# A hybrid encoder layer: V stored once in token order, stores of attention results moved to another queue, the first norm placed elsewhere

## The chip, the core and the metric

The kernel runs on one core of a Trainium2 chip. A core has five engines that run their own instruction streams side by side and wait for each other by semaphores: TensorE (PE: matrix products and transposes, with its weight load shown as PEld), VectorE (DVE), ScalarE (ACT), GpSimd (POOL) and SyncE (SP). Data moves between DRAM and the on-chip memory by DMA; in this kernel DMAs are issued by SP and, for some stores, by ACT. Each engine takes its instructions in order, and a DMA issue that has to wait holds up what stands behind it on the engine that issues it. PE writes to eight banks of a small accumulation memory (PSUM), from which DVE and ACT fetch the results.

The metric is the device time of one launch in microseconds (us).

## The reference

One encoder layer with one batch of 2048 tokens and 1024 features, in float32:

```python
y = rmsnorm(h, norm_mix_g) @ w_in                      # q, k, v: 8 heads of 64; a, g: 512 each
att = dilated_sliding_attention(rot(q), rot(k), v)     # three patterns, mixed by their denominators
conv = silu(layernorm(depthwise_conv31(a * sigmoid(g))))
h = h + concat([att, conv]) @ w_out
h = h + cross_attention(rmsnorm(h), rmsnorm(mem))      # 4 heads of 256, 256 memory rows
h = h + square(relu(rmsnorm(h) @ w_up)) @ w_down       # 4096 wide
out = rmsnorm(h, norm_final_g)
```

The three patterns are `(128, 1), (512, 4), (2048, 16)`: in each, a token attends to those up to 64 steps away on both sides, where a step is 1, 4 or 16 tokens. The results of the three patterns are added with weights that come from a softmax over their log-denominators.

## The kernel before

Every matrix product is made of three: each operand is split into a high part that PE takes exactly and a low remainder, and `mm3` (L204) adds high x high, high x low and low x high. The splitting is the work of ACT (`ACT.copy`) and DVE or POOL (the subtraction). With a free size of 512 such a product is 24 matmuls for 1024 rows of weights.

The program goes through these stages:

- Up to about 230 us: the products of the memory rows with the cross attention's weights, and the normalised transposed x, kept as high and low parts for four quarters of 512 tokens.
- Up to about 405 us: the projections of q and k (`lin_qk`) and the gated input of the convolution (`glu`, for the first two quarters of the tokens). Beside them `vscale` (L517) computes a scale for every 128 features of V: it sums squares of the weights on POOL (L526, L527), and in the next step PE adds them up over partitions (L533). Each `yield` is a place where `weave` may give another generator its turn; `vscale` has two for each of its four rounds, and a rate of 0.3 rounds per step of the main line.
- 405 to 557 us: `lin_v` (L543), V for two groups of four heads in 16 tiles of 128 tokens each, with `glu` between and after. A tile is 24 matmuls, an ACT cast to half precision (L571), a DVE subtraction (L572) and stores. A row of V (`VR`, 1040 half-precision numbers) has for each head 64 high parts, two ones and 64 low parts. The tile `vst` (8 buffers) goes to DRAM three times, once for each pattern in the order in which the pattern reads it: `vscr3` by one DMA from SP, `vscr2` by four from ACT, `vscr1` by two from SP, so seven DMAs for each tile.
- About 557 to 905 us: attention of quarter 0 (`att(0, p2_)`, L1029). Pattern 3 (step 16) is done here for the whole sequence (`att_far`), patterns 1 and 2 for the first quarter. Into this stage are woven the first layer norm of the convolution (`conv_ln(0)`, L1030: one of its steps after each of the first nine steps of attention) and then the rest of `glu` for the last two quarters (`rest`, 0.8 steps per step of attention).
- After that, for each of the four quarters, `post(p)`: output projection, cross attention, MLP and final norm, with the attention of the next quarter and its convolution woven in.

Attention works in units. A far unit (`att_far.unit`, L820) takes four of the 16 residues of one head: PE writes scores to two banks (L829, L830), DVE adds the mask and takes the minimum into column 65 of the result tile (`att_probs`, L762), ACT exponentiates (L763); a step later PE transposes (L769), ACT and DVE split into high and low (L772, L773); a step later PE multiplies with V (L777 to L779), DVE or ACT copies the result (L841, L839) and SP stores it to `oscr` (L842). `att` (L989) keeps three units in flight and takes two steps of the woven generators for each. The result tile of a far unit is `o3` with three buffers, so a unit can't begin to write its minimum before the store of the third unit before it has landed. A near unit does the same with pattern 2 (`pat` 1) and pattern 1 (`pat` 0); the result of pattern 2 for a pair of heads (`o1`, one buffer) is stored by SP (L962), that of pattern 1 stays on the chip.

When a pair of heads is through, `combine` (L851) loads the stored results of patterns 2 and 3 back (`ld`, by two DMAs from SP), waits two steps and then mixes them on DVE, POOL and ACT. At the same time `load_v` (L916) fetches V for the next pair of heads: one DMA for pattern 3 (in quarter 0 only), two for pattern 2, one for pattern 1; each of these tiles has one buffer. `far_keys` (L802) loads the keys of a head for pattern 3 as a whole, 16 x 160 with edges; `far_q` (L807) loads the high and the low part of q, and POOL copies the high part to the other 64 partitions.

The order of the instructions on each engine is not simply that of the program text: a planner in the framework simulates the program and puts each engine's instructions in an order by its own estimates of when they are ready. `pinned` and `after` (L78, L83) tell it to issue a step's work not before a named earlier instruction.

`conv_ln` (L225) takes the tiles that its caller gives it through `alloc`; for the first norm these are the eight buffers `t2`, which `glu` uses too.

Of the kernel before, what the change touches and what calls it, by code (L numbers as in the profile page):

```python
# [47 lines left out]
def hybrid_layer(ctx, tc, A, out):  # L48
# [61 lines left out]
    vscr1 = dr.tile([17, 16, 8, VR], F16, name="vscr1")  # L110
    vscr2 = dr.tile([4, 5, 4, 32, VR], F16, name="vscr2")
    vscr3 = dr.tile([16, P, VR], F16, name="vscr3")
# [404 lines left out]
    def vscale():  # L517

        for pr in range(4):
            sq = [t2(f"vsq{pr}{q}", F32, (P, 4, P)) for q in range(2)]  # L520
            for q in range(2):
                dma(sq[q], wcols(w_in, 2 * DATT + P * pr, rows=(4 * q, 4 * q + 4)))
            for k in range(KC):
                w = sq[k // 4][:, k % 4]
                ACT.activation(w, w, AF.Square, scale=gain("mix", k))
            POOL.tensor_tensor(sq[0], sq[0], sq[1], op=ALU.add)  # L526
            POOL.tensor_tensor(sq[0][:, 0:2], sq[0][:, 0:2], sq[0][:, 2:4], op=ALU.add)  # L527
            yield
            with ExitStack() as st:
                after(st, "pe", "dve")  # L530
                pc = ps("c", f"vss{pr}")
                for q in range(2):
                    PE.matmul(pc[:, 0:1], sq[0][:, q], ones[:, 0:1], start=q == 0, stop=q == 1)  # L533
                v = top.tile([P, 4], F32, tag="vs", name=f"vs{pr}", bufs=2)
                DVE.tensor_scalar(v[:, 0:1], pc[:, 0:1], 1e-30, None, op0=ALU.max)
                POOL.tensor_tensor(v[:, 1:2], v[:, 0:1], mhalf, op=ALU.pow)
                DVE.tensor_scalar(v[:, 2:3], v[:, 1:2], 512.0, None, op0=ALU.mult)
                DVE.tensor_scalar(vmul[:, pr:pr + 1].bitcast(I32), v[:, 2:3].bitcast(I32), 0x7F800000, None,
                                  op0=ALU.bitwise_and)
                DVE.reciprocal(vinv[:, pr:pr + 1], vmul[:, pr:pr + 1])  # L540
            yield

    def lin_v(g, ns):  # L543
# [18 lines left out]
        for t in range(4 * ns[0], 4 * ns[-1] + 4):  # L562
# [5 lines left out]
            st = lbv.tile([P, 4, VW], F16, tag="vst", name=f"vst{g}_{t}", bufs=8)  # L568
# [6 lines left out]
            dma(vscr3[:, 8 * t:8 * t + 8, gs].rearrange("r i e -> i r e"), s2)  # L575
            c2, i2 = divmod(PADI + 8 * t, 32)
            for b in range(4):
                dma(vscr2[b, c2, :, i2:i2 + 8, gs].rearrange("a i e -> i a e"), s2[b:P:4], nc.scalar)
            for e in range(2):
                dma(vscr1[t + e, :, 4 - 4 * e:8 - 4 * e, gs].rearrange("r i e -> i r e"), s2[64 * e:64 * e + 64])  # L580
# [116 lines left out]
    def edges():  # L697
        zrow = wp.tile([16, 1, VR], F16, tag="raw", name="zrow", bufs=2)
        DVE.memset(zrow, 0.0)
        zb = zrow.to_broadcast([16, 4, VR])  # L700
        for b in range(4):
            dma(vscr2[b, 0, :, 0:PADI, :].rearrange("a i e -> i a e"), zb)
            dma(vscr2[b, 4, :, PADI:, :].rearrange("a i e -> i a e"), zb)
        dma(vscr1[0, :, 0:4, :], zb)
        dma(vscr1[16, :, 4:8, :], zb)
# [24 lines left out]
    with ExitStack() as st:  # L730
        lbk = pool("lin_k", stack=st)
        cu = pool("conv0", stack=st)
        conv0 = pinned(conv_units(cu, 0, (0, 1)), "dve")
        weave(islice(steps, 31), (vsc, 0.3), (conv0, 0.5))
        drain(vsc, conv0)
        next(steps)
# [65 lines left out]
    def far_keys(p2_, h):  # L802
        k = p2_.tile([P, 16, 160], F32R, tag="k3", name=f"k3_{h}", bufs=2)
        dma(f(k.rearrange("p r i -> p (r i)")), f(kscr[:, :, h].rearrange("x d r i -> (x d) (r i)")))
        return k

    def far_q(h, e):  # L807
# [3 lines left out]
        for x, d in ((0, t), (1, ql)):  # L811
            dma(f(d[0:64]), f(qfar[x, :, h, 8 * e:8 * e + 8, :].rearrange("d r i -> d (r i)")))
        POOL.tensor_copy(t[64:P], f(t[0:64]))
        return t, ql

    def att_far(p2_, h, k, vt, q):

        pr, hh = divmod(h, 2)

        def unit(rq, qh, ql):  # L820
            os_ = p2_.tile([P, 4, ROW], F32, tag="o3", name=f"o3_{h}{rq}", bufs=3)
# [20 lines left out]
            dma(oscr[pr][1].rearrange("(p r) (h e) -> p r h e", r=16, h=2)[:, 4 * rq:4 * rq + 4, hh], os_)  # L842
# [8 lines left out]
    def combine(p, pr, o0):  # L851
# [6 lines left out]
        yield  # L858
        sm_ = top.tile([P, 5, 8], F32, tag="csm", name=f"csm{p}{pr}")
# [49 lines left out]
    def att_units(p, far, then):  # L909
# [6 lines left out]
        def load_v(pr):  # L916
            es = slice(pr * 2 * VW, (pr + 1) * 2 * VW)
            if far:
                vt[2] = far.tile([P, 16, 2 * VW], F16, tag="v3", name=f"v3_{pr}")
                dma(vt[2], vscr3[:, :, es].rearrange("r i e -> i r e"))  # L920
            vt[1] = aq.tile([P, 4, 2, 2 * VW], F16, tag="v2", name=f"v2_{p}{pr}")
            for c in range(2):
                dma(vt[1][:, :, c], vscr2[:, p + c, :, :, es].rearrange("b a i e -> (a i) b e"))
            vt[0] = aq.tile([P, 5, 2 * VW], F16, tag="v1", name=f"v1_{p}{pr}")
            dma(vt[0], vscr1[4 * p:4 * p + 5, :, :, es].rearrange("c r i e -> (r i) c e"))

        def unit(pr, hh, pat, g, k, q_, os_, opt):
# [33 lines left out]
            if g and hh and pat:  # L961
                dma(oscr[pr][0][512 * p:512 * (p + 1)].rearrange("(p b) e -> p b e", b=4),  # L962
                    os_.rearrange("p b h e -> p b (h e)"))
# [53 lines left out]
    with ExitStack() as st:  # L1017
        p2_ = pool("att_far", stack=st, side="right")
        p2_.tile([P, 16, 160], F32R, tag="k3", name="k3", bufs=2)
        qlow3 = low_parts(p2_, 1024, 2, "ql3")  # L1020
        p2_.tile([P, 200], F32, name="farpad")
# [3 lines left out]

        def ln_alloc(role, dtype, name, shape=(P, 512)):
            return top.tile(list(shape), F32, tag="cl_" + role, name=name) if role[:3] == "col" else t2(name, dtype)

        first = pinned(att(0, p2_), "pe")  # L1029
        weave(islice(first, 9), (pinned(conv_ln(0, ln_alloc), "pe"), 1))  # L1030
        weave(first, (rest, 0.8))
# [291 lines left out]
```

## Time and profile before

| what | value |
|---|---|
| median of three runs | 3071.7 us (3071.03 to 3072.67) |
| the profiled execution's own time | 3069.8 us |
| its span, from the first to the last instruction | 3068.0 us |
| PE busy | 2908.4 us (95% of the span) |
| DVE, ACT, POOL busy | 1853.8, 1198.6, 416.9 us |
| mean granted clock of PE | 0.973 |
| DMA packets and data | 612871, 440.54 MB |

The profile is one execution of the program, recorded by the hardware. A line of the page names the engine, the line of the kernel (L205 is line 205), the tile that is written and those that are read; a wait names the instruction or the DMA that ended it. SPq and ACTq are the issues of DMAs by these engines, with the time that an issue took on the engine. Matmuls are pipelined and overlap, so the distance between starts tells more than the length of one. The page cuts the span into 40 slices of 76.7 us and gives the busy share of each in tenths; PEclk is the share of its full clock that PE was granted.

### The profile page before, as it was taken

The numbers are of one execution on the slowest core, as the hardware profiler recorded it, in microseconds if no ns is written. First come the engines' busy times: TensorE is split into PE (matmuls) and PEld (weight loads), VectorE is DVE, ScalarE is ACT, GpSimd is POOL, SyncE is SP. The second block draws the span as 40 slices with busy tenths as digits, with TensorE's granted clock in tenths as the row PEclk, the third lists the DMA queues.
The fourth block names the chain that finished last, engine by engine and source line by source line (L and its number), as shares of the span: only waits on it lengthen the run. The fifth ranks groups of instructions, "written<-read, shape, count | busy, mean of one in ns | idle before, by whom it ended". The sixth has DMA issues, their size and how long they took to land.

```text
span 3068.0 us, 43093 instructions
## 1 busy us (share of the span) xinstructions
PE 2908.4 (95%) x16396; PEld 2479.3 (81%) x16396; DVE 1853.8 (60%) x3295; ACT 1198.6 (39%) x2002; POOL 416.9 (14%) x486
## 2 busy tenths in 40 slices
PE   8989998677779999999999999999999999999999
PEld 8878798566668888888888888888888888988888
DVE  6545534344466777666768776666967656554445
ACT  5633211355533533343443344344433444432332
POOL 2336411212110011120001101100100120000000
PEclk9999999699889999999999999999999999999999
DMA  8878855556472444455434445453534355233332
GB/s 270 281 166 202 198 142 152 173 142 164 124 215 90 132 124 136 126 157 163 139 114 131 120 138 150 140 177 109 139 109 134 111 156 174 83 96 97 96 97 76
DMA packets 612871, 440.54 MB, mean 144 GB/s; under 512 B 191461, under 2 KB 541721, under 8 KB 611640
## 3 DMA queue, kind: packets, MB, share of 16 engines
q1 hardware_dynamic: 588056, 424.08, 48.5%
q10 hardware_dynamic: 24608, 13.71, 1.7%
q8 instruction: 129, 2.11, 0.3%
q14 instruction: 78, 0.64, 0.1%
HBM read 337.27 MB, written 100.42 MB: 143 GB/s over the span
## 4 chain that ended last, share of the span: by engine, by line
PE 72%; DMA 6%; DVE 5%; ACT 2%; issue 1%; ACTq 0%; SPq 0%; POOL 0%; POOLq 0%; DVEq 0%
PE dn L205 7%; PE up L205 7%; PE up L207 7%; PE up L206 7%; PE dn L207 7%; PE dn L206 7%; DMA vscr<-vst 3%; PE s L942 2%; PE pt L769 2%; PE xs L205 2%; PE xs L207 2%; PE xs L206 2%; PE x L205 2%; PE x L207 2%; PE x L206 2%; PE o L206 2%
## 5 line engine op out<-in xcount | busy, mean ns | idle before, releaser
L206 PE MATMUL dn<-hhl,whi_d 128*128 128x512 f32 (+1 forms) x1056 | 403.2, 384 | 2.8 <-DVE hhl L1201 2.8
L205 PE MATMUL up<-mh,whi_u 128*128 128x512 f32 x1024 | 402.3, 393 | 0.5 <-DVE rl L1198 0.5
L207 PE MATMUL dn<-hhh,wlo_d 128*128 128x512 f32 (+1 forms) x1056 | 402.7, 384 | 0.0
L205 PE MATMUL dn<-hhh,whi_d 128*128 128x512 f32 (+1 forms) x1056 | 400.4, 392 | 0.0
L207 PE MATMUL up<-mh,wlo_u 128*128 128x512 f32 x1024 | 399.3, 390 | 0.0
L206 PE MATMUL up<-ml,whi_u 128*128 128x512 f32 x1024 | 398.8, 389 | 0.0
L219 DVE SCALAR_TENSOR_TENSOR cacc<-cu,cw,cacc 128x512 f32<-128x512 f32 x480 | 384.1, 802 | 6.2
L196 ACT CAST whi_d<-raw_d 128x1024 fp32r<-128x1024 f32 x128 | 134.6, 1052 | 392.0 <-PE up L206 383.7
L1216 DVE TENSOR_TENSOR h<-h,dn 128x512 f32<-128x512 f32 (+1 forms) x264 | 172.2, 667 | 190.9 <-PE dn L207 190.3
L196 ACT CAST whi_u<-raw_u 128x1024 fp32r<-128x1024 f32 x128 | 134.6, 1052 | 371.3 <-PE dn L206 332.4
L763 ACT ACTIVATE sm<-sm,o 128x256 f32<-128x256 f32 (+1 forms) x384 | 172.7, 469 | 216.9 <-DVE o L762 213.6
L1198 DVE SCALAR_TENSOR_TENSOR rl<-up,ssumx 128x512 f32<-128x512 f32 x128 | 87.9, 690 | 238.6 <-PE up L207 235.2
L207 PEld LDWEIGHTS dn<-hhh,wlo_d 128*128 128x128 f32 x1056 | 198.5, 188 | 39.5
L206 PEld LDWEIGHTS dn<-hhl,whi_d 128*128 128x128 f32 x1056 | 198.8, 188 | 38.6 <-DVE hhl L1201 3.4
L205 PEld LDWEIGHTS dn<-hhh,whi_d 128*128 128x128 f32 x1056 | 198.0, 188 | 38.8 <-DVE h L1216 3.2
L207 PEld LDWEIGHTS up<-mh,wlo_u 128*128 128x128 f32 x1024 | 192.3, 188 | 39.9
L205 PEld LDWEIGHTS up<-mh,whi_u 128*128 128x128 f32 x1024 | 192.2, 188 | 38.6 <-DVE rl L1198 0.9
L206 PEld LDWEIGHTS up<-ml,whi_u 128*128 128x128 f32 x1024 | 192.5, 188 | 38.0
L762 DVE CUSTOM_DVE_ANT_0 sm<-s,mask 128x256 f32<-128x256 f32 (+1 forms) x384 | 139.9, 376 | 123.0 <-PE s L942 83.2
L197 DVE TENSOR_TENSOR wlo_d<-raw_d,whi_d 128x1024 fp32r<-128x1024 f32 x128 | 161.2, 1259 | 19.5 <-ACT whi_d L196 19.3
L197 DVE TENSOR_TENSOR wlo_u<-raw_u,whi_u 128x1024 fp32r<-128x1024 f32 x128 | 161.2, 1259 | 8.9 <-ACT whi_u L196 8.9
L205 PE MATMUL xs<-whi_a,yh 128*128 128x256 f32 x512 | 149.6, 293 | 8.8 <-ACT xp L1159 6.0
(386 smaller groups left out, 6575.3 us busy)
## 6 DMA issues: line engine op xcount, KB each, us to landing
raw_u<-in_w_up_dram SPq DMA_DIRECT2D x128, 512.0 KB
raw_d<-in_w_down_dram SPq DMA_DIRECT2D x128, 512.0 KB
raw_o<-in_w_out_dram SPq DMA_DIRECT2D x32, 512.0 KB
raw_a<-ascr SPq DMA_DIRECT2D x32, 512.0 KB
raw_b<-bscr SPq DMA_DIRECT2D x32, 512.0 KB
k<-kscr SPq DMA_DIRECT2D x24, 512.0 KB
k<-kscr SPq DMA_DIRECT2D x8, 1280.0 KB
ld<-oscr SPq DMA_DIRECT2D x32, 264.0 KB
```

The lines of the kernel that those rows point to most:

```text
L196: ACT.copy(hi, raw)
L197: (lo_eng or DVE).tensor_tensor(lo, raw, f(hi), op=ALU.subtract)
L205: PE.matmul(o, lh, rh, start=first, stop=False)
L206: PE.matmul(o, lh, rl, start=False, stop=False)
L207: last["pe"] = PE.matmul(o, ll, rh, start=False, stop=end)
L219: DVE.scalar_tensor_tensor(acc, u[:, t:t + 512], cw[:, c, t:t + 1], acc, op0=ALU.mult, op1=ALU.add)
L762: last["dve"] = DVE.tensor_tensor_reduce(dst, so, mask[:, 256 * m:256 * m + nk], 1.0, 3e38, ALU.add, ALU.min, mn)
L763: last["act"] = ACT.activation(dst, dst, AF.Exp, bias=mn, scale=-1.0)
L769: last["pe"] = PE.transpose(pt[:, j, :], sm[:, j, :], ident)
L942: last["pe"] = PE.matmul(o, q_[x][:, qs], kv, start=x == 0, stop=x == 1)
L1198: last["dve"] = DVE.scalar_tensor_tensor(r, pt, 0.0, rsb, op0=ALU.max, op1=ALU.mult)
L1216: last["dve"] = DVE.tensor_tensor(hs[m][:, sl], hs[m][:, sl], pt, op=ALU.add)
```

## The change

It has six parts.

- V is stored once, in the order of the tokens, in `vtok` (2048 rows with 256 zero rows on each side): one DMA for each tile, from SP, and six buffers `vst` instead of eight. The patterns pick their rows when V is loaded: pattern 2 by eight DMAs for each pair of heads instead of two, pattern 1 by five instead of one, pattern 3 by one as before. The zero edges are two DMAs instead of ten.
- The results of far units are collected by two in tiles of eight residues (three buffers) and stored by one DMA of ACT's queue for two units. The results of pattern 2 are stored by ACT's queue too, in all four quarters.
- `combine` waits one step more in quarter 0.
- The high part of the far q is loaded twice instead of copied by POOL, and the far keys are loaded without the last 16 of each 160 columns.
- The first norm takes the tiles `ld`, `cth`, `ctl` and `cat`, which `combine` uses later, instead of five of the `t2`, and is spread over the first 25 steps of attention; the rest of `glu` starts with the first step, at 0.78 per step.
- `vscale` has three steps in a round instead of two, and a rate of 0.42.

```diff
-    vscr1 = dr.tile([17, 16, 8, VR], F16, name="vscr1")
-    vscr2 = dr.tile([4, 5, 4, 32, VR], F16, name="vscr2")
-    vscr3 = dr.tile([16, P, VR], F16, name="vscr3")
+    vtok = dr.tile([256 + S + 256, VR], F16, name="vtok")
...
             POOL.tensor_tensor(sq[0][:, 0:2], sq[0][:, 0:2], sq[0][:, 2:4], op=ALU.add)
             yield
+            yield
...
-            st = lbv.tile([P, 4, VW], F16, tag="vst", name=f"vst{g}_{t}", bufs=8)
+            st = lbv.tile([P, 4, VW], F16, tag="vst", name=f"vst{g}_{t}", bufs=6)
...
-            dma(vscr3[:, 8 * t:8 * t + 8, gs].rearrange("r i e -> i r e"), s2)
-            c2, i2 = divmod(PADI + 8 * t, 32)
-            for b in range(4):
-                dma(vscr2[b, c2, :, i2:i2 + 8, gs].rearrange("a i e -> i a e"), s2[b:P:4], nc.scalar)
-            for e in range(2):
-                dma(vscr1[t + e, :, 4 - 4 * e:8 - 4 * e, gs].rearrange("r i e -> i r e"), s2[64 * e:64 * e + 64])
+            dma(vtok[256 + P * t:256 + P * (t + 1), gs], s2)
...
-        zb = zrow.to_broadcast([16, 4, VR])
-        for b in range(4):
-            dma(vscr2[b, 0, :, 0:PADI, :].rearrange("a i e -> i a e"), zb)
-            dma(vscr2[b, 4, :, PADI:, :].rearrange("a i e -> i a e"), zb)
-        dma(vscr1[0, :, 0:4, :], zb)
-        dma(vscr1[16, :, 4:8, :], zb)
+        zb = zrow.to_broadcast([16, 16, VR])
+        for t0 in (0, 256 + S):
+            dma(vtok[t0:t0 + 256].rearrange("(q x) e -> q x e", q=16), zb)
...
-        weave(islice(steps, 31), (vsc, 0.3), (conv0, 0.5))
+        weave(islice(steps, 31), (vsc, 0.42), (conv0, 0.5))
...
-        k = p2_.tile([P, 16, 160], F32R, tag="k3", name=f"k3_{h}", bufs=2)
-        dma(f(k.rearrange("p r i -> p (r i)")), f(kscr[:, :, h].rearrange("x d r i -> (x d) (r i)")))
+        k = p2_.tile([P, 16, 144], F32R, tag="k3", name=f"k3_{h}", bufs=2)
+        dma(f(k), f(kscr[:, :, h].rearrange("x d r i -> (x d) r i")[:, :, 0:144]))
...
-        for x, d in ((0, t), (1, ql)):
-            dma(f(d[0:64]), f(qfar[x, :, h, 8 * e:8 * e + 8, :].rearrange("d r i -> d (r i)")))
-        POOL.tensor_copy(t[64:P], f(t[0:64]))
+        for x, d in ((0, t[0:64]), (0, t[64:P]), (1, ql[0:64])):
+            dma(f(d), f(qfar[x, :, h, 8 * e:8 * e + 8, :].rearrange("d r i -> d (r i)")))
...
-            os_ = p2_.tile([P, 4, ROW], F32, tag="o3", name=f"o3_{h}{rq}", bufs=3)
+            if rq % 2 == 0:
+                o8[0] = p2_.tile([P, 8, ROW], F32, tag="o3", name=f"o3_{h}{rq}", bufs=3)
+            o2 = o8[0]
+            os_ = o2[:, 4 * (rq % 2):4 * (rq % 2) + 4]
...
-            dma(oscr[pr][1].rearrange("(p r) (h e) -> p r h e", r=16, h=2)[:, 4 * rq:4 * rq + 4, hh], os_)
+            if rq % 2:
+                dma(oscr[pr][1].rearrange("(p r) (h e) -> p r h e", r=16, h=2)[:, 4 * rq - 4:4 * rq + 4, hh], o2,
+                    nc.scalar)
...
         yield
         yield
+        if p == 0:
+            yield
...
-                dma(vt[2], vscr3[:, :, es].rearrange("r i e -> i r e"))
+                dma(vt[2], vtok[256:256 + S, es].rearrange("(i r) e -> i r e", r=16))
...
-                dma(vt[1][:, :, c], vscr2[:, p + c, :, :, es].rearrange("b a i e -> (a i) b e"))
+                src = vtok[512 * (p + c):512 * (p + c) + 512, es].rearrange("(i a b) e -> b a i e", a=4, b=4)
+                for b in range(4):
+                    dma(vt[1][:, b, c], src[b])
...
-            dma(vt[0], vscr1[4 * p:4 * p + 5, :, :, es].rearrange("c r i e -> (r i) c e"))
+            for c in range(5):
+                t0 = 256 + 512 * p + P * c - 64
+                dma(vt[0][:, c], vtok[t0:t0 + P, es].rearrange("(i r) e -> r i e", r=16))
...
                 dma(oscr[pr][0][512 * p:512 * (p + 1)].rearrange("(p b) e -> p b e", b=4),
-                    os_.rearrange("p b h e -> p b (h e)"))
+                    os_.rearrange("p b h e -> p b (h e)"), nc.scalar)
...
+        c01 = []
+
         def ln_alloc(role, dtype, name, shape=(P, 512)):
-            return top.tile(list(shape), F32, tag="cl_" + role, name=name) if role[:3] == "col" else t2(name, dtype)
-
+
+            if role[:3] == "col":
+                return top.tile(list(shape), F32, tag="cl_" + role, name=name)
+            if role in ("cs0", "cs1"):
+                if not c01:
+                    c01.append(aq.tile([P, 2, 512], F32, tag="ld", name="lc01"))
+                return c01[0][:, int(role[2])]
+            if role in ("cs2", "cs3", "sum"):
+                return aq.tile(list(shape), F32, tag={"cs2": "cth", "cs3": "ctl", "sum": "cat"}[role], name=name)
+            return t2(name, dtype)
+
+        ln0 = pinned(conv_ln(0, ln_alloc), "pe")
         first = pinned(att(0, p2_), "pe")
-        weave(islice(first, 9), (pinned(conv_ln(0, ln_alloc), "pe"), 1))
-        weave(first, (rest, 0.8))
+        weave(islice(first, 25), (ln0, 0.33), (rest, 0.78))
+        drain(ln0)
+        weave(first, (rest, 0.78))
         drain(rest)
```

More of the change, by code (lines that the diff above doesn't have):

```diff
@@ L818, in att_far @@
         pr, hh = divmod(h, 2)
+        o8 = {}
         def unit(rq, qh, ql):
-            os_ = p2_.tile([P, 4, ROW], F32, tag="o3", name=f"o3_{h}{rq}", bufs=3)
+            if rq % 2 == 0:
+                o8[0] = p2_.tile([P, 8, ROW], F32, tag="o3", name=f"o3_{h}{rq}", bufs=3)
+            o2 = o8[0]
+            os_ = o2[:, 4 * (rq % 2):4 * (rq % 2) + 4]
             sm = wk.tile([P, 4, P], F32, tag="sm", name="sm", bufs=3)
@@ L1018, in hybrid_layer @@
         p2_ = pool("att_far", stack=st, side="right")
-        p2_.tile([P, 16, 160], F32R, tag="k3", name="k3", bufs=2)
+        p2_.tile([P, 16, 144], F32R, tag="k3", name="k3", bufs=2)
         qlow3 = low_parts(p2_, 1024, 2, "ql3")
-        p2_.tile([P, 200], F32, name="farpad")
+        p2_.tile([P, 176], F32, name="farpad")
         rest = pinned(pipeline(*(u for c in range(4) for u in glu(c, (2, 3), True))), "pe")
```

## The prediction

> **What bounds the kernel now.** First the page's slices: who is busy, at which clock, and what the chain that ended last is made of.
>
> ```profile
> PE   8989998677779999999999999999999999999999
> ...
> PEclk9999999699889999999999999999999999999999
> ...
> PE 72%; DMA 6%; DVE 5%; ACT 2%; issue 1%; ACTq 0%; SPq 0%; POOL 0%; POOLq 0%; DVEq 0%
> ```
>
> TensorE (PE) is the bound nearly everywhere; slices 8 to 12 (about 540 to 920 us) are the exception. So I asked for the busy time in stretches around them (columns: stretch, length, busy time of PE, weight load, DVE, ACT and POOL with counts, granted clock, DMA share, GB/s):
>
> ```profile
> 500.00:557.00 57.00, 43.28 (x294) 39.97 (x293) 24.71 (x39) 3.97 (x13) 5.08 (x11) 0.88 0.52 152
> ...
> 570.00:613.00 43.00, 23.32 (x132) 20.52 (x133) 19.66 (x64) 21.92 (x42) 10.41 (x8) 0.57 0.51 150
> 613.00:872.00 259.00, 199.48 (x1605) 168.09 (x1604) 112.48 (x449) 133.76 (x284) 43.84 (x64) 0.92 0.58 155
> ...
> 951.00:3068.00 2117.00, 2093.17 (x11352) 1774.99 (x11352) 1385.49 (x2289) 826.22 (x1286) 166.39 (x219) 1.00 0.43 126
> ```
>
> The end of V, the first norm and the attention of quarter 0 leave PE idle for 14, 20 and 60 us, at a lowered clock; after 951 us only 24 of 2117 us are idle. Only what moves these three stretches counts. PE's waits say what ends the idle time (total, times, longest):
>
> ```profile
> PE s L829 <- DVE o L762: 39.7, 31, 6.7
> ...
> PE lin L205 <- DVE vst L572: 13.5, 2, 12.4
> ...
> PE lps0m L239 <- DVE lsum L244: 8.4, 1, 8.4
> PE lps0v L239 <- DVE lsum L255: 6.3, 1, 6.3
> ...
> PE vss L533 <- POOL vsq L527: 5.6, 2, 4.0
> ```
>
> Behind DVE stands something else each time. In V it is ScalarE (ACT), by the timeline of its queue:
>
> ```profile
> 521.36 20.55 ACTq L57 DMA_DIRECT2D vscr<-vst  x20
> 541.96 1.20 ACT L571 CAST vst<-v 128x256 f16<-128x256 f32 x4 [22.23 <-DMA vscr<-vst]
> ```
>
> ACT issued 20 stores in 20.55 us, 1.03 each, where one alone takes 0.584: in the trace's records the kernel's DMAs take turns on eight semaphores, so each issue waits until the eighth before it, whatever its queue, has landed (some 3.9 us). The cast behind them came 22 us late and PE had no bank. In the far units it is a store's landing, by DVE's timeline:
>
> ```profile
> 668.16 0.20 DVE L865 TENSOR_TENSOR csm<-ld 128x8 f32<-128x8 f32 x1 [3.19 <-DMA ld<-oscr]
> 670.65 0.29 DVE L762 CUSTOM_DVE_ANT_0 sm<-s,mask 128x128 f32<-128x128 f32 x1 [2.08 <-DMA oscr<-o]
> ...
> 704.18 0.29 DVE L762 CUSTOM_DVE_ANT_0 sm<-s,mask 128x128 f32<-128x128 f32 x1 [4.24 <-DMA oscr<-o]
> ```
>
> **The change part by part**, against the profiled execution's 3069.8 us (span 3068.0 and 1.8 around it), which is 1.9 below the median 3071.7.
>
> V's stores (A). 224 stores (7 for each of 32 tiles; 128 of them ACT's, 75 us of issue at 0.584) become 32 on SP. Four ACT issues at 1.03 are 4.1 us a tile against PE's 24 matmuls at 0.12 = 2.9, so stores set the pace now; afterwards ACT's cast (0.385) and DVE's subtraction (0.418) fit in 2.9. PE's idle time in this stretch that ends at vst or at the sigmoid behind it is 0.95+1.10+1.20+12.36+0.95 = 16.6. The lowered clock costs 43.3 x 0.12 = 5.2 more, of which I take half: -19. Ends 0 (the first keys are late instead) and -22. Next late is POOL's wvl (3.4 us of PE idle at 481), untouched. Six buffers instead of eight last 17 us against a landing of 4.
>
> First norm (B). PE's idle time around it is 8.35+6.28+2.77+1.59 = 19.0, and the clock of 0.57 costs 23.3 x 0.43 = 10. Filling the gaps with the glu steps, which now start at once and at 0.78 end at step 123 instead of 129, could win 29. But the norm's own work stays on two engines in order: DVE 6 x 0.69 + 8 x 0.68 = 9.6, ACT 4 x 0.63 + 4 x 0.81 + 4 x 0.61 + 2 table loads of 1.28 = 10.8. Every unit passes both, so I leave two thirds of 20.4 on the path: 29-14 = -15. Ends 0 and -29. Its rooms are free before the first sum of patterns needs them: eight resumptions at 0.33 are over by step 25, the sum comes after 16 units, or 32 steps.
>
> On the clock the Trainium skill (TensorE: Matmul & The Clock Gate, Part 1) says that an idle window of about 3.4 us halves the rate until a busy one has passed. The trace agrees: in the stretch at 0.57 matmuls of 512 columns follow each other in 0.43 us, elsewhere in 0.23. By its rule 37 of the 43 us were at half rate and cost 18.5, so B would be -24 and the time 3010.
>
> Far results (C). PE waits 1.48+5.84+4.41+4.84+2.19+6.66+2.23+4.61 = 32.3 us where DVE waits for oscr or ld. Three tiles of eight rows instead of three of four give a store three units' time instead of one, and its issue no longer stands behind SP's loads. A unit without such a wait still shows up to 1.47 (at 629), so 8 x 1.3 = 10 stays: -22. Of the clock's 199.5 x 0.08 = 16 half goes: -8. The costs: 16 far and 4 distance-4 stores on ACT in this quarter, 20 x 0.584 = 11.7, half of it behind other work: +6. The casts and exponentials queue behind each issue, and PE's transposes wait for them. And ld's second load stands behind the next pair's V loads, now 13 or 14 instead of 3 or 4: 10 x 0.54 of SP's issue = 5.4 at three pair changes, 16, less the step of 1.8 us that combine now waits anyway: +11. Sum -13. Ends -30 and +23 (nothing won, the issues in full).
>
> vscale (D). A step later the sums of squares are there: 5.6 us of idle time goes, I take -6; ends 0 and -8. Its twelve resumptions at 0.42 fit in the 31 steps.
>
> V's loads and ACT's stores in quarters 1 to 3 (E). 12 pairs x 10 more issues at SP's 0.47 = 56 us, and 12 stores on ACT, 7. Cover: a distance-4 load issued at 1011.55 has its first reader at 1046.9; weights are two raw and four split tiles ahead, at 24 x 0.227 = 5.4 us each 33 us. I take 0; without cover +63. The pieces carry the same rows of 520 bytes as before.
>
> Far q and k (F). 16 POOL copies (1.06 each) and POOL's 140 us of waiting for qh go, 16 issues (0.45 = 7 on SP) come; far keys in rows of 576 instead of 10240 bytes, 2048 packets near 0.03 us over 16 engines, 4 us against 3. Hidden: loads come a head ahead. 0; ends -5 (POOL's wlo delayed less) and +7. The two zero stores instead of ten lie beside PE's work at a full clock: 0.
>
> Sum: -19-15-13-6 = -53, so 3016.8 for an execution like the profiled one and 3018.7 for the median.
>
> **The rivals.**
> (1) The far stage keeps its time: the pair's 13 loads hold up ld as the stores did, and the norm's work eats half its gain. For it: ld alone held DVE for 7.08 us at 808, in just such a burst. Then A, D and half of B remain, -32: 3039.
> (2) All waits go: -22-29-30-8 = -89 gives 2983. For it: no engine is over 8 tenths busy there. Against it: PE's waits of 0.5 to 1.5 at nearly every unit, which are not DMA's.
> (3) Slower: ACT itself now waits for the eighth DMA before its store to land. For it: the 22.23 us above are this wait. Against it: that took 2 DMAs per us, where the attention has 0.6, and only bursts reach it. At 4.65 us (the landing of the store that held DVE at 704) instead of the 0.3 taken, 20 stores cost 87 more: 3106. It decides from 53/20 = 2.65 us each.
> (4) V's loads are not covered: 63 us on SP against -53 is +10: 3082. Against it the covers in E.
> For (4) speaks a rule of the Trainium skill (DMA: Bandwidth & Descriptors, Rules for kernel authors): coalesce small transfers, since under 64 KB one pays mostly overhead. A piece of V is 65 KB; the trace agrees in kind, 32 and 65 KB stores both landing in about 3.9 us.
> (5) The change does nothing: the planner that orders the queues puts other waits in the same places: 3072.
>
> **How the numbers follow.** Forecast 0.50 (its own range, from A and B at their lower ends, 17 less, to a quarter of A, B and C missing, 12 more: 3002 to 3031), (1) 0.22, (2) 0.12, (3) 0.10, (4) 0.03, (5) 0.03. About 0.2%, 6 us, is what a measurement can tell from no change. Faster is the forecast, (1) and (2), 0.84; same 0.03; slower (3) and (4), 0.13. I say 3019. A range from 2980 to 3062 takes in (1) and most of (2) and leaves out (3), (4), (5) and a third of (2), 0.20.
>
> **What would show it.** A: no wait of PE for vst over 2 us, ACT's casts every 2.9 us, 32 stores. B: no lps wait over 3 us, and a clock near 0.9 where it was 0.57. C: no wait of DVE for oscr over 2 us; if ACT's time before an exponential ends at a DMA instead, rival 3 has come. D: no wait for vsq. E: the last 2117 us unchanged within 5. The prediction is wrong if quarter 0's attention is as long as now, or if PE waits for v in the later quarters.

## The result, and the profile after

The changed kernel takes 2992.7 us (median of four runs, 2992.2 to 2995.7), the kernel before 3071.4 in the same comparison: a ratio of 0.9749 with a 95% interval of 0.9732 to 0.9766. That is 79 us less by the medians and 77 by the ratio, where 53 were forecast. The time lies in the range given (2980 to 3062), but 26 us below the forecast, outside the forecast's own narrower range (3002 to 3031), and nearer to rival 2 (2983) than to it.

The page of the kernel after, the same three lines as before: PE in slices of 74.8 us, its granted clock, and the chain that ended last.

```profile
PE   8999999888899999999999999999999999999999
...
PEclk9999999899999999999999999999999999999999
...
PE 87%; DVE 6%; DMA 3%; ACT 2%; issue 1%; SPq 1%; POOL 0%; POOLq 0%; DVEq 0%; ACTq 0%
```

The slices with a 6 or a 7 are gone, and of those with a clock below 9 tenths one is left. DMA's share of the chain is halved, PE's is up from 72% to 87%. The span is 2990.4 us, the mean clock 0.986.

For the account by stages I cut both profiled executions at PE's own milestones: first matmul of V, first score of a far unit, transposes of the ninth unit, first matmul of the output projection. Units come by heads, four far and four near ones for each, so the stretch up to the ninth unit's transposes holds the first head (the expectations below say "the eighth unit"), and the one behind it the other 56 units of the quarter, far and near; I call that stretch the far units, after those whose tiles were changed. The stretches of before in these cuts (columns as in the prediction: stretch, length, busy time of PE, weight load, DVE, ACT, POOL, clock, DMA share, GB/s):

```profile
405.90:568.80 162.90, 142.73 (x963) 132.40 (x962) 62.68 (x100) 18.85 (x44) 24.59 (x38) 0.94 0.52 153
568.80:625.60 56.80, 35.20 (x229) 30.34 (x228) 27.15 (x95) 29.28 (x58) 10.50 (x8) 0.67 0.50 155
625.60:876.20 250.60, 192.25 (x1538) 161.99 (x1536) 108.89 (x433) 131.01 (x277) 43.84 (x64) 0.90 0.60 158
```

And the same stages after:

```profile
395.30:535.20 139.90, 137.71 (x964) 129.85 (x963) 63.49 (x103) 21.41 (x44) 25.02 (x39) 0.99 0.48 137
535.20:575.80 40.60, 33.09 (x248) 28.30 (x247) 21.57 (x88) 24.46 (x50) 3.40 (x2) 0.92 0.50 126
575.80:798.80 223.00, 178.88 (x1492) 151.57 (x1489) 104.77 (x421) 131.69 (x276) 36.43 (x56) 0.93 0.74 192
```

V: PE is idle for 2.2 us instead of 20.2. The norm: 40.6 us instead of 56.8, with 19 matmuls more in it. The far units: 44.1 us idle instead of 58.4, and 46 matmuls fewer, since some of them came earlier, and some of the next quarter's later.

The waits after (us in total, times, longest):

```profile
PE s L945 <- DVE o L753: 31.0, 36, 3.5
...
PE s L824 <- DVE o L753: 15.5, 30, 2.5
...
DVE csm L864 <- DMA ld<-oscr: 3.7, 1, 3.7
...
PE v L204 <- POOL wvl L559: 2.2, 1, 2.2
```

There is no row any more in which PE waits for `vst`, for the norm's sums (`lps`) or for `vss`, and none in which DVE waits for a far result's store, as it did before:

```profile
DVE sm L762 <- DMA oscr<-o: 19.1, 8, 4.7
```

What PE waits for in the units is DVE's minimum, 0.5 (far, L824) and 0.9 us (near, L945) on average and 3.5 at the longest. The wait for `wvl` that is left stands at the head of V (398 us), on the first group's weights; the one of 3.4 us that the prediction spoke of, on the second group's, is gone.

### The profile page after: what moved, and what is told of

Read it like the earlier page. It is cut to its first block, busy times and chain, and to the rows that moved or that the text cites. A ratio compares the mean times of both kernels' runs of the same rounds, so it can differ in the third digit from the quotient of the medians.

```text
span 2990.4 us, 42736 instructions
## 1 busy us (share of the span) xinstructions
PE 2886.1 (97%) x16396; PEld 2462.7 (82%) x16396; DVE 1840.1 (62%) x3295; ACT 1200.2 (40%) x2002; POOL 398.6 (13%) x470
## 4 chain that ended last, share of the span: by engine, by line
PE 87%; DVE 6%; DMA 3%; ACT 2%; issue 1%; SPq 1%; POOL 0%; POOLq 0%; DVEq 0%; ACTq 0%
PE up L203 8%; PE dn L203 8%; PE up L205 8%; PE up L204 8%; PE dn L205 7%; PE dn L204 7%; PE lin L203 3%; PE lin L204 3%; PE lin L205 3%; PE s L945 2%; PE x L203 2%; PE xs L203 2%; PE pt L760 2%; PE x L205 2%; PE x L204 2%; PE xs L205 2%
## 5 line engine op out<-in xcount | busy, mean ns | idle before, releaser
L217 DVE SCALAR_TENSOR_TENSOR cacc<-cu,cw,cacc 128x512 f32<-128x512 f32 x480 | 377.9, 789 | 5.3
```

The source lines that it names most:

```text
L217: DVE.scalar_tensor_tensor(acc, u[:, t:t + 512], cw[:, c, t:t + 1], acc, op0=ALU.mult, op1=ALU.add)
```

## The experiments

Two sets of runs tell the parts apart: each part alone in the kernel before, and the kernel after with one thing undone or enlarged. A limit holds for all of them: the planner orders the whole program anew with every edit, so stretches that an edit doesn't touch move by a few us as well. The stretch behind the far units, the same work in all, differs by up to 11 us between the profiled executions of the parts. It takes 2191.6 us after, and 2192.6 to 2201.8 in the kernels below that undo one thing elsewhere, so after is at the short end there. Ratios are therefore read to about 5 us, and a variant that is 4 or 5 us slower than after isn't told from it.

**The parts alone.** The first part of V:

```diff
+    vtok = dr.tile([256 + S + 256, VR], F16, name="vtok")
...
+            dma(vtok[256 + P * t:256 + P * (t + 1), gs], s2)
...
+                for b in range(4):
+                    dma(vt[1][:, b, c], src[b])
```

> The kernel before with V stored once and picked on loading, nothing else. Theory 1, the parts add up and each gains in its own stage: from the first V matmul to the first far score the two traces differ by 23.0 us (162.9 before, 139.9 after), and this kernel shows all of it: 3071.4 - 23 = 3048. Theory 2, the longer bursts of V loads on SP collide with the far stores that still stand in SP's queue here: the same 23 are won in the V stage, but some 10 are given back between the eighth unit and the output projection (250.6 us before), 3058, and VectorE's waits for oscr grow from 19 us.

The norm's rooms (their lines are those of the change above) and its place in the steps:

```diff
-        weave(islice(first, 9), (pinned(conv_ln(0, ln_alloc), "pe"), 1))
-        weave(first, (rest, 0.8))
+        weave(islice(first, 25), (ln0, 0.33), (rest, 0.78))
+        drain(ln0)
+        weave(first, (rest, 0.78))
```

> The kernel before with only the first norm in the other tiles, spread over 25 steps, and the rest of glu at 0.78 from the first step. Theory 1: the stage from the first far score to the eighth unit's transposes shrinks by 16 as in the whole change (56.8 to 40.6 us) and nothing else moves: 3055. Theory 2, the norm's gain depends on V's: without it the norm's loads still stand behind V's stores on SP and arrive late, the gain is half, 3063.

The results of far units in tiles of eight on ACT's queue, with the pattern 2 stores there, the additional step and the shorter keys:

```diff
+            if rq % 2 == 0:
+                o8[0] = p2_.tile([P, 8, ROW], F32, tag="o3", name=f"o3_{h}{rq}", bufs=3)
...
+            if rq % 2:
+                dma(oscr[pr][1].rearrange("(p r) (h e) -> p r h e", r=16, h=2)[:, 4 * rq - 4:4 * rq + 4, hh], o2,
+                    nc.scalar)
```

> The kernel before with only the far results in eights and both result stores on ScalarE's queue (with the combine step more and the far keys of 144 columns, which make the room). Theory 1: the stage from the eighth unit to the output projection shrinks by 27 as in the whole change (250.6 to 223.1 us): 3044. Theory 2, the costs that the prediction put on this part are real (6 us for ScalarE's issues; the 11 for ld behind V's longer burst do not arise here) and the rest of the 27 came from the norm and from V: 3071.4 - 24 = 3047 at best, 3058 if only the eight waits go and nothing else.

And `vscale`:

```diff
             yield
+            yield
...
-        weave(islice(steps, 31), (vsc, 0.3), (conv0, 0.5))
+        weave(islice(steps, 31), (vsc, 0.42), (conv0, 0.5))
```

> The kernel before with only the third step in a round of vscale and the rate 0.42. Theory 1: all that the whole change gains before the first V matmul (405.9 to 395.3 us) is this: 3061, no wait of TensorE for vsq, and no half clock around 240 and 320 us. Theory 2, the prediction's term: 5.6 us of idle time and little of the clock, 3065; the other 4 us come from shorter queues elsewhere.

What came out, each against before. The stages are differences in us between the profiled executions; the ratio comes from the timed runs, and the last column is the ratio less one, times 3071.4.

| kernel | to first V matmul | V | norm, 8 units | far units | the rest | ratio (95% interval) | us |
|---|---|---|---|---|---|---|---|
| V alone | -5.3 | -26.9 | -1.7 | +2.1 | +5.9 | 0.9898 (0.9878 to 0.9917) | -31 |
| norm alone | -0.5 | +2.2 | -12.2 | +2.9 | +10.8 | 0.9982 (0.9971 to 0.9994) | -6 |
| stores alone | -3.0 | -0.7 | +1.8 | -31.6 | +4.4 | 0.9910 (0.9891 to 0.9928) | -28 |
| vscale alone | -9.6 | -0.1 | +1.1 | 0.0 | +2.4 | 0.9979 (0.9969 to 0.9988) | -6 |
| all (after) | -10.6 | -23.0 | -16.2 | -27.5 | -0.2 | 0.9749 (0.9732 to 0.9766) | -77 |
| forecast | -6 | -19 | -15 | -13 | 0 | | -53 |

Each part works mainly in its own stage; -31, -6, -28 and -6 make -71 of the -77, and as each of them is known to 3 to 6 us, the parts add up within what can be told. The first column is less sharp: V alone and the stores alone move it by 5.3 and 3.0 us without an edit there. The stage of V in the kernel with V alone, and its far units:

```profile
400.60:536.60 136.00, 136.00 (x964) 128.33 (x963) 62.82 (x100) 21.44 (x44) 24.63 (x40) 1.00 0.47 136
...
591.70:844.40 252.70, 192.66 (x1529) 162.18 (x1527) 107.91 (x433) 130.51 (x276) 43.95 (x64) 0.89 0.58 154
```

PE has no idle time in V at all, and its 964 matmuls took 136.0 us busy instead of 142.7, as the clock is full. The far units take 2.1 us more. As the second theory had it, DVE's waits for their stores did grow, from 19.1 to 30.5 us in twelve waits, beside V's loads in 13 or 14 pieces; its waits for `ld` fell from 13.4 to 10.8, and PE is idle for only 1.7 us more. The part makes fewer stores and takes them off ACT's queue at once; which of the two did it was not separated. The wait for POOL's `wvl`, which I had left standing, went too. ACT's queue of before shows why:

```profile
460.55 13.55 ACTq L57 DMA_DIRECT2D vscr<-vst  x15
474.15 0.60 ACT L508 ACTIVATE sig<-lin 128x512 f32<-128x512 f32 x1 [13.48 <-DMA vscr<-vst]
474.64 1.98 ACT L559 CAST wvh<-raw_v 128x1024 fp32r<-128x1024 f32 x2
```

`wvh`, from which POOL makes `wvl`, stood behind 13.55 us of store issues. With V alone its first cast starts at 459.14.

The far units with the stores alone:

```profile
623.80:842.80 219.00, 182.93 (x1537) 154.23 (x1535) 108.30 (x432) 129.03 (x276) 43.78 (x64) 0.97 0.72 176
```

1537 matmuls against 1538; PE is idle for 36.1 us instead of 58.4 (-22.3), and busy for 9.3 less at a clock of 0.97 instead of 0.90.

The norm alone is the part that did not hold. Its two stretches, and two of its waits:

```profile
570.40:615.10 44.70, 35.01 (x248) 29.98 (x247) 21.69 (x88) 24.76 (x50) 5.47 (x4) 0.85 0.43 113
615.10:868.50 253.40, 180.98 (x1493) 153.82 (x1490) 105.28 (x422) 132.97 (x276) 48.82 (x68) 0.90 0.61 163
```

```profile
PE s L829 <- DVE o L762: 52.6, 31, 9.5
...
DVE sm L762 <- DMA oscr<-o: 23.0, 10, 9.4
```

It is 12 us ahead after eight units. The next stretch then takes 2.9 us more than before although it holds 45 matmuls fewer: PE's waits for the far units' minimum rose from 39.7 to 52.6 us, and those of DVE for the stores from 19.1 to 23.0.

**Room or queue?** The far stores changed in two ways, larger tiles and another queue. Back on SP's queue, the tiles of eight kept:

```diff
-                dma(oscr[pr][1].rearrange("(p r) (h e) -> p r h e", r=16, h=2)[:, 4 * rq - 4:4 * rq + 4, hh], o2,
-                    nc.scalar)
+                dma(oscr[pr][1].rearrange("(p r) (h e) -> p r h e", r=16, h=2)[:, 4 * rq - 4:4 * rq + 4, hh], o2)
...
-                    os_.rearrange("p b h e -> p b (h e)"), nc.scalar)
+                    os_.rearrange("p b h e -> p b (h e)"))
```

> The changed kernel with both result stores issued by SP again; the tiles of eight stay. Theory 1, the room decides (three tiles of eight give a store three units' time instead of one) and the queue hardly matters: 2993 to 2996. Theory 2, the queue decides: the stores stand behind the V bursts in SP's order, VectorE's waits for oscr come back at the three pair changes, 5 us each, and ld comes later: 3005. By the prediction's term of 6 us for ScalarE's issues it would even be faster, 2987.

On ACT's queue, but in three tiles of four:

```diff
-            if rq % 2 == 0:
-                o8[0] = p2_.tile([P, 8, ROW], F32, tag="o3", name=f"o3_{h}{rq}", bufs=3)
-            o2 = o8[0]
-            os_ = o2[:, 4 * (rq % 2):4 * (rq % 2) + 4]
+            os_ = p2_.tile([P, 4, ROW], F32, tag="o3", name=f"o3_{h}{rq}", bufs=3)
...
-            if rq % 2:
-                dma(oscr[pr][1].rearrange("(p r) (h e) -> p r h e", r=16, h=2)[:, 4 * rq - 4:4 * rq + 4, hh], o2,
-                    nc.scalar)
+            dma(oscr[pr][1].rearrange("(p r) (h e) -> p r h e", r=16, h=2)[:, 4 * rq:4 * rq + 4, hh], os_,
+                nc.scalar)
```

> The changed kernel with the far results in three tiles of four again, one store for each unit, but on ScalarE's queue. Theory 1, the room decides: a store lands some 6 us after its issue on this queue in the changed kernel, longer than a unit of 3.6, so most of the eight waits return, 15 to 25 us: 3008 to 3018. Theory 2, the queue decides: the stores land in time because nothing stands before them: 2993 to 2997.

With the stores on SP the ratio is 0.9755 (0.9739 to 0.9771), the same as after within what can be told. In its profiled execution (3009.5 us, the longest of four) DVE waits 3.9 us for far results' stores, in four waits, and the far units take 226.9 us, 3.8 more than after. In fours on ACT it is 0.9865 (0.9847 to 0.9884): 36 us of the gain are gone, most of them in the far units, which take 254.1 us instead of 223.0, and the waits are back:

```profile
PE s L821 <- DVE o L753: 51.2, 32, 9.2
...
DVE sm L753 <- DMA oscr<-o: 33.9, 9, 9.0
```

So the room decides, and the queue weighs some 4 us at most. That holds for fours as well: with V alone they are stored from SP beside the same V loads (and the norm as before), and the far units take 252.7 us, against 254.1 here from ACT. With fours they are even slower than before (250.6). That it is the room and not the halved number of stores, the next run shows.

**Do ACT's issues cost anything?** Each far store cut into four issues on ACT, 48 more:

```diff
+                for z in range(4):
+                    zs = slice(2 * z, 2 * z + 2)
+                    dma(oscr[pr][1].rearrange("(p r) (h e) -> p r h e", r=16, h=2)[:, 4 * rq - 4 + 2 * z:4 * rq - 2 + 2 * z, hh],
+                        o2[:, zs], nc.scalar)
```

> The changed kernel with each of the 16 far stores cut into four issues on ScalarE, 48 issues more at 0.366 us (the median in the changed kernel), 17.6 us of ScalarE in the attention of quarter 0. Theory 1, ScalarE's issues lie beside other work: 2993 to 2995. Theory 2, half of them is on the path, as the prediction's term has it: 3001; where they also wait for the eighth DMA before them to land, more.

The ratio is 0.9750 (0.9736 to 0.9765), and the far units take 223.3 us against 223.1: no cost. What rival 3 spoke of does happen now, in one row of ACT's waits, twice, and still costs nothing that shows:

```profile
ACT sm L754 <- DMA oscr<-o: 9.3, 2, 7.2
```

**The norm beside the new stores.** The kernel after with the norm as before, in the `t2` tiles again (only the lines of its place in the steps are shown):

```diff
-        weave(islice(first, 25), (ln0, 0.33), (rest, 0.78))
-        drain(ln0)
-        weave(first, (rest, 0.78))
+        weave(islice(first, 9), (pinned(conv_ln(0, ln_alloc), "pe"), 1))
+        weave(first, (rest, 0.8))
```

> The changed kernel with the first norm as before (in the t2 tiles, one step after each of the first nine steps of attention, glu's rest at 0.8 after that). Alone the norm's part gained 17 us up to the first transposes and gave nearly all back in the far units, 5.5 in the end. Theory 1, it gave them back to the waits for oscr, which the stores' part takes away: here undoing it costs the 17: 3009. Theory 2, the norm's work and glu's steps are only moved within the stage, so it is worth as little here: 2998.

0.9762 (0.9748 to 0.9777): 4 us more than after by the ratio, 9 by the medians (3001.8, where the kernel before took 3073.1 beside it), with intervals that overlap. Its stages:

```profile
536.90:590.00 53.10, 35.55 (x230) 30.69 (x229) 27.64 (x95) 29.28 (x58) 8.44 (x6) 0.68 0.50 134
590.00:809.50 219.50, 184.53 (x1528) 155.49 (x1526) 107.61 (x433) 129.52 (x276) 31.40 (x52) 0.96 0.76 189
```

The norm's part takes 12.5 us from the first stretch (53.1 to 40.6) and adds 3.5 to the second (219.5 to 223.0). That is 9 us for both together, and in the kernel before it was 12.2 and 2.9, also 9.

**Is it the glu steps that are merely moved?** My theory by then was that the glu matmuls fill the norm's gaps and are missing later. So their rate was changed, with the end at the same step:

```diff
-        weave(islice(first, 25), (ln0, 0.33), (rest, 0.78))
+        weave(islice(first, 25), (ln0, 0.33), (rest, 0.4))
         drain(ln0)
-        weave(first, (rest, 0.78))
+        weave(first, (rest, 0.88))
```

> The kernel after the change with the remaining glu steps at 0.40 per step of attention in the first 25 steps (beside the norm) and 0.88 afterwards, so that they end at the same step, 123. Ten of its 96 steps move from the norm's surroundings to the units behind. My theory now of why the norm's part alone won 17 us at the first transposes and kept about 5: glu's matmuls are filler, and what fills the norm's gaps is missing later. By it the first transposes come later here (up to 8 us: ten steps of glu at some 0.8 us of PE each), most of it is won back by the output projection, and the time is 2993, within 4. The rival: a gap beside the norm is worth its whole length, and the units behind had no room for more filler: +8, 3001.

The time is that of after (0.9748, 0.9731 to 0.9765), but not by the way I had written: the transposes did not come later, but 0.5 us earlier after the first score (6.8 us instead of 7.3). These "first transposes", here and in the expectation, are those of the second unit. PE's matmuls of glu alone (tile `lin`; stretch, length, PE's busy time, clock, DMA share, GB/s) from there to half way (the transposes of the 33rd unit) and on to the output projection, after:

```profile
542.50:681.80 139.30, 49.20 (x144) 0.88 0.64 168
681.80:798.80 117.00, 41.49 (x136) 0.98 0.77 197
```

and with the late glu steps:

```profile
541.60:672.50 130.90, 43.04 (x133) 0.90 0.70 177
672.50:800.40 127.90, 46.87 (x150) 0.94 0.74 187
```

With eleven glu matmuls fewer (6.2 us of PE) the first of these is 8.4 us shorter, and with 14 more (5.4 us) the other is 10.9 longer; with the stretch ahead it is 263.6 and 265.6 us in all. Where these steps stand didn't matter to the total. Nor do they account for what the norm's part gives back. All of PE's work from the first score to the second unit's transposes and from there to half way, with the old norm and after:

```profile
536.90:559.10 22.20, 11.04 (x49) 0.57 0.37 96
559.10:681.00 121.90, 102.32 (x828) 0.91 0.73 183
...
535.20:542.50 7.30, 6.12 (x39) 1.00 0.81 225
542.50:681.80 139.30, 109.63 (x854) 0.88 0.64 168
```

The second stretch grew by 17.4 us, 7.3 of them PE's busy time (5.5 glu's) and 10.1 idle time. The first one lost 10.0 of idle time (11.2 to 1.2). So the idle time beside the norm was not filled but moved: from the first score to the output projection PE idles for 52.5 us with the old norm and for 51.6 after (79.9 and 82.1 in the kernel before and with the norm alone). What is kept is busy time, 212.0 us instead of 220.1, at a mean clock of 0.93 instead of 0.91 and with 19 matmuls of the next quarter now behind the output projection's start. The idle time came back as PE's waits for DVE's minimum, 27.1 us in the second stretch instead of 18.4, where ACT and DVE are now busy 7.5 and 4.4 us longer; neither kernel has a wait for a store. That the norm's own passes through ACT and DVE are what holds the minimum up is argued from these rows, not shown by a run.

**V's loads.** Every piece cut in two by heads, 416 issues instead of 208 (the expectation counted 16 too few); pattern 2 is shown, pattern 1 likewise:

```diff
-                    dma(vt[1][:, b, c], src[b])
+                    for z in range(2):
+                        zs = slice(z * VW, (z + 1) * VW)
+                        dma(vt[1][:, b, c, zs], src[b][:, :, zs])
```

> The kernel after the change (2993 us), with every load of V for patterns 1 and 2 cut in two by heads: 400 issues on SP instead of 208, in pieces of 33 KB with rows of 260 bytes. This doubles just what part E and rival 4 speak of. If the loads are covered (E), quarters 1 to 3 stay as they are (2118 us after 872, within 5), and only the three pair changes of quarter 0 can feel it, where a result's load stands behind 26 pieces instead of 13: the wait for ld, 3.7 us once now, may grow to some 10 at each of three changes, so 2993 to 3015. If the loads are not covered (rival 4), 192 more issues at 0.47 on SP show as +90: 3083.

0.9766 (0.9749 to 0.9783): 5 us more than after, at the edge of what can be told, where 208 uncovered issues at 0.47 would have made 98. The far units with their three pair changes, and the rest, in this kernel:

```profile
578.00:798.70 220.70, 176.54 (x1492) 149.82 (x1489) 104.66 (x422) 131.65 (x276) 36.47 (x56) 0.94 0.80 194
798.70:3000.30 2201.60, 2167.94 (x11720) 1836.68 (x11720) 1435.95 (x2380) 858.60 (x1336) 183.09 (x236) 0.99 0.44 127
```

After, the far units take 223.0 us, so the pair changes cost nothing that shows, and DVE's wait for `ld` did not grow (2.7 us in two waits). The rest takes 10 us more than after's 2191.6, where I had allowed 5; kernels whose edit leaves that stretch alone reach 2201.8, so the 10 can't be put down to the loads, nor cleared of them.

**The additional step of `combine`.**

```diff
-        if p == 0:
-            yield
```

> The kernel after the change without the additional step of combine in quarter 0. My sum had +11 for ld's second load behind the next pair's V loads, with the step of 1.8 us already taken off. If that queue matters, DVE waits 1.8 us longer for ld at each of three pair changes, from 3.7 us once now to some 9 in all: 2998. If the load has landed before its reader in any case, nothing changes: 2993, within 3.

0.9793 (0.9779 to 0.9808): 14 us more than after, well above the 5 expected; 7.8 of them are there when the output projection starts, the others behind that. Both kernels ask for the second half of `ld` between V's pieces (SP's queue without the step):

```profile
610.62 0.42 SPq L57 DMA_DIRECT2D ld<-oscr  x1
611.10 7.40 SPq L57 DMA_DIRECT2D v<-vtok  x7
618.55 0.70 SPq L57 DMA_DIRECT2D ld<-oscr  x1
```

and DVE's read of it waits 5.90 without the step:

```profile
623.73 0.17 DVE L862 TENSOR_TENSOR csm<-ld 128x8 f32<-128x8 f32 x1 [5.90 <-DMA ld<-oscr]
```

against 3.72 after. In all DVE waits 9.2 us for `ld` instead of 3.7. So the queue in front of `ld` is real (seven pieces took 7.40 us of SP), and the step is what hides most of it. In the far units alone, 232.0 us instead of 223.1, it costs 8.9 and not the 5.5 that DVE waits: PE waits there 25.9 us instead of 13.6 for the far units' minimum, and 17.1 instead of 23.3 for the near ones'. The others lie in the stretch behind, which this edit leaves alone and which moves by as much in other kernels; they can't be put down to the step.

**The copy of the far q by POOL again:**

```diff
-        for x, d in ((0, t[0:64]), (0, t[64:P]), (1, ql[0:64])):
-            dma(f(d), f(qfar[x, :, h, 8 * e:8 * e + 8, :].rearrange("d r i -> d (r i)")))
+        for x, d in ((0, t), (1, ql)):
+            dma(f(d[0:64]), f(qfar[x, :, h, 8 * e:8 * e + 8, :].rearrange("d r i -> d (r i)")))
+        POOL.tensor_copy(t[64:P], f(t[0:64]))
```

> The kernel after the change with the high part of the far q copied by POOL again (16 copies near 1.06 us, 16 issues fewer on SP): part F undone. If it is hidden, as I took it: 2993, within 4. If POOL's waiting for qh holds up POOL's remainders of the weights beside the attention, up to +5 (my end for that): 2998; if SP's 16 issues had cost something, up to -7: 2986.

0.9765 (0.9750 to 0.9779): 5 us more than after, with intervals that overlap. The far units took 1.4 us more (224.5), while the output projection starts 1.4 us earlier than after; the difference arises behind it, in stretches that this edit doesn't touch. Whether the part is worth 0 or 5 stays open.

## Why the prediction was right or wrong

**The whole:** right in sign and place, and too small by a third. Two terms were too small (V's stores and the far results) and one too large (the norm), so the errors offset each other in part: with the norm at the 6 us that it gave alone, the sum would be some 35 us off instead of 26. That the time lies in the range is owed to its width, drawn to take in two rivals.

**V's stores, -19 forecast, -27 in the stage alone (-23 in the whole change) and -31 in all (25 to 37 by the interval).** The mechanism held: no wait for `vst`, casts every 2.9 us after. The step that failed is the account of what would stay. I took 16.6 us of the idle time, left POOL's `wvl` standing as the next late thing, and credited half of the clock. With V alone all 20.2 us of idle time went, since that `wvl` was late because ACT's cast for it stood in the same queue of stores, and so did all of the clock's loss (6.7 us of busy time). A wait that I took for a neighbour was a child of the one removed. The other stretches, without an edit, moved by -5.3 and +5.9 us, so nothing more is read from the difference of 27 and 31.

**The first norm, -15 forecast, -6 alone, 4 to 9 beside the rest.** The first sign I had named came (no `lps` wait, the clock at 0.92 instead of 0.67), and the gain at the second unit's transposes was 19 us in the whole change. The step that failed is the sum of 29 to be won less 14: what the first stretch gives is 12, and the units behind it take 3 back. I had counted 19 of the 29 as idle time that glu's steps would fill. Over the whole of the quarter's attention idle time fell by 0.9 us beside the new stores and rose by 2.2 alone; the 9 us won there are PE's busy time (8.1 and 11.5 us less), in the main by the clock (0.91 to 0.93, and 0.86 to 0.89 alone). The Trainium skill's rule on the clock (TensorE: Matmul & The Clock Gate, Part 1) made this part -24. The trace agrees with the rule for the clock itself, 1.00 in the 7.3 us up to the second unit's transposes after, with 1.2 of them idle, where 26.3 us before, with 15.2 idle, had 0.56. But a stretch at full clock is no gain where its work comes back as length elsewhere, and here the measured time, some 4 to 9 us, decides against the -24.

**Far results, -13 forecast, -28 measured.** The two gains were sized right, -22 and -8 against -22.3 and -9.3. What failed is both costs. ACT's issues (+6) are free: 48 more of them changed nothing. The queue in front of `ld` (+11 after the step) left 3.7 us of waiting at one pair change of three, since the step of `combine`, which I had valued at 1.8 us each time (5.4 in all), is worth 9 in the far units. And my reading that a store also suffers from standing behind SP's loads carried little: with the stores on SP the ratio is the same and the far units take 3.8 us more. The room of eight rows does most of it, 31 us in the far units.

**vscale, -6 forecast, -6 measured (4 to 10 by the interval).** No wait for `vsq` is left. The equal number is in part luck: in its stage PE's idle time fell by 2.8 us, not 5.6, and its busy time by 6.8, of which 4 to 5 also show in kernels without this edit.

**V's loads, 0 forecast.** The rest behind the far units took 0.2 us less than before (2191.6 us), and the doubled pieces cost some 5 us by the ratio, not 98. The Trainium skill's rule that small transfers should be coalesced, as under 64 KB one pays mostly overhead (DMA: Bandwidth & Descriptors, Rules for kernel authors), is not refuted by that: SP did need 1.10 us per piece in the burst after (seven in 7.69 us). But the overhead lay on an engine on whose queue, with the step of `combine`, little depended (one wait of 3.7 us for `ld`), and so has hardly a price here; without the step it has one.

**Far q and keys, 0 forecast:** 0 to 5, open.

**The rivals.** (1) fell: the far units took 27.5 us less. (2) was nearest: in the far units all of DVE's waits on DMA but one of 3.7 us did go. What keeps the time 10 us above it is the norm: by stages the change gave 10.6, 23.0, 16.2 and 27.5 us, where this rival had 8, 22, 29 and 30. (3) fell: after, no wait of ACT in the attention ends at a store of results, whose issues took 0.34 to 0.40 us each, and in the kernel that did have such waits, up to 7.2 us long, they cost nothing that shows. (4) fell with the doubled loads, (5) with the result.

## What to carry to other kernels

Before naming what is late next, ask whether it stands in the same queue as the work that is removed: then it goes with it. When a buffer's release waits for a store, count the units that the buffers last before moving the store to another queue; here 36 us hung on the rows of a tile and at most some 4 on the queue. Gaps that are closed by bringing work forward or spreading it count only after the stretches that it came from or went to have been added, all cut at the same milestones: the idle time may only have moved.

## What was unexpected of the hardware

- A DMA's issue on ACT took 0.34 to 0.40 us for the 20 stores of results between 535 and 800 us after, where a store of V, by which I had priced them, took 0.584. On SP the seven pieces of V between two loads of `ld` took 7.40 to 7.69 us, 1.06 to 1.10 each, where I had taken 0.47 to 0.54.
- Halving V's pieces raised the DMA engines' busy share in the far units from 0.74 to 0.80, at 192 and 194 GB/s, and the stretch took no longer (223.0 and 220.7 us).
- The granted clock's loss is part of a wait's price: in V, 20.2 us of idle time cost 6.7 us more in the matmuls around it, in the far units 22.3 cost 9.3.
